# A transformer block on one core: the last head's norm by Newton steps, a conditioning row kept in a scratch row, and no separate square-root activation

## The chip, the core and the metric

The kernel runs on one core of one Trainium2 chip. The time is device microseconds of one execution; less is better. The engines are called as in the profile: PE multiplies matrices (PEld is its weight load), DVE and ACT do elementwise work, POOL does a little, SP issues the DMAs.

## The reference

One layer of a diffusion backbone: 512 latent tokens and 256 context tokens of width 1024. Everything is float32.

```python
mod = silu(c) @ w_mod + b_mod                 # six vectors of 1024: shift, scale, gate, twice
h   = rmsnorm(x) * (1 + sc1) + sh1            # the context the same, with c_ctx
# one projection of h feeds two mixers
o_mla  = attention of 4 heads over context + latent keys (128 plain + 64 rotary features)
o_hgrn = rmsnorm(forward scan + backward scan, 4 heads of 128) * silu(gate)
x = x + gt1 * (concat(o_mla, o_hgrn) @ w_out)
h2 = rmsnorm(x) * (1 + sc2) + sh2
x = x + gt2 * ((silu(h2 @ w_gate) * (h2 @ w_up)) @ w_down)
return rmsnorm(x) * g_final
```

## The kernel before

Features lie on the partitions and tokens along the free axis, except where a product needs it the other way. Each float32 operand is split into a rounded part and a remainder (`hi` and `lo`, `wh` and `wl`, and so on), and each product is three matmuls (`mm3`, lines 150 to 152). Weights arrive in units of 128x1024 through a ring of three buffers (`wf`); ACT casts a unit to `wh` (line 132) and DVE forms the remainder `wl` (line 133).

The stages follow each other: squares and norm of the inputs with the first two modulation vectors; the projection of the values; the low-rank attention features; four heads of the recurrence, each with two directions (`hgrn_dir`) and an output part (`hgrn_out`); the rotary key (`mla_kpe`, line 709); values, rotary queries and plain queries of the attention (`make_v`, `make_qr`, `make_q`, lines 770 to 803); the attention; the output projection; the second norm; the feed-forward part; the last norm.

The parts around the change:

- `rstd_cols` (line 184) makes 1/sqrt(mean + eps) of a few columns. With `fast=True` ACT takes the square root (line 190), DVE the reciprocal and one Newton step (lines 180 to 182). Otherwise DVE makes a first guess from the bits (lines 196 to 198) and takes three Newton steps.
- `hgrn_out(h)` adds up a head's output in PSUM (`po`), squares it on ACT (line 610), takes `rstd_cols`, with `fast` for the last head alone, and scales into `ow` (line 614), which PE transposes (line 620). ACT and DVE store the result as `onh` and `onl` (lines 622, 623).
- `late_mod` (line 422) makes the four later modulation vectors without PE: 32 rows of weights are fetched into the same `wf` ring (in the trace `wl<-in_wmt_dram`), and DVE multiplies each with silu(c) and sums (line 427). silu(c) lies on all partitions in `scx`, which is the place of the cosine and sine tables in `cs`. So it is made twice: once ahead of the recurrence (lines 433 to 435) for the first 12 rows; then the tables are loaded over it (line 746), and when the rotary queries are done, `c` is fetched again, goes through the sigmoid on ACT (line 814) and is multiplied on DVE (line 815).
- ACT needs a table for each of Exp, Sigmoid, Sqrt and Silu, and the compiler puts a table load (ACT_TABLE_LOAD) where the function changes. Copies, casts, scalings and squares need no load. Some small activations are there for their table alone, among them line 818 (Exp of one column), meant to stand ahead of the softmax, and line 1037 (Sqrt of one column), which stands in the code ahead of the last norm.
- The order in which an engine runs its instructions isn't the order of the code: a scheduler places each instruction on its engine's list by a priority, which follows the code, and by a model of when its inputs are there. Line 1037 depends on nothing late, so it lands in the middle of the program. Once the list is made, each engine works through it in order, and so does the DMA queue on SP.

Of the kernel before, what the change touches and what calls it, by code (L numbers as in the profile page):

```python
# [10 lines left out]
F32 = mybir.dt.float32  # L11
# [3 lines left out]
AF = mybir.ActivationFunctionType  # L15
# [3 lines left out]
P = 128  # L19
DM = 1024  # L20
# [4 lines left out]
NH = 4  # L25
# [27 lines left out]
def block_kernel(ctx: ExitStack, tc: tile.TileContext, xT, ctxT, vec, cin, cst, msk, wm, wmt, wi, wqkv, wo, wgu, wd, out):  # L53
    nc = tc.nc

    def pool(name, side, bufs=1):
        return tc.alloc_tile_pool(name=name, bufs=bufs, side=side, reuse_waits="tile")
# [4 lines left out]
    def nm(s):  # L62
        uid[0] += 1
        return f"{s}_{uid[0]}"
# [4 lines left out]
    def sm():  # L69
        return psum.tile([P, 512], F32, tag="sm", name=nm("sm"), bufs=4)  # L70
# [16 lines left out]
    epst = L0.tile([P, 1], F32, name="epst")  # L87
# [3 lines left out]
    epst2 = L0.tile([P, 1], F32, name="epst2")  # L91

    def V(name):
        a, b = VC[name]
        return vc[:, a:b]

    def C(name):
        a, b = CC[name]
        return cs[:, a:b]
# [44 lines left out]
    def unit(i, ahead=2):  # L144
        prefetch(i + 1 + ahead)
        return made[i]
# [12 lines left out]
    def tick(n=1):  # L159
        for _ in range(n):  # L160
            for g in list(side[:3]):
                if next(g, 1):
                    side.remove(g)
# [14 lines left out]
    def newton(r, t, v, n):  # L178
        for _ in range(n):
            nc.vector.tensor_mul(t, r, r)  # L180
            nc.vector.scalar_tensor_tensor(t, t, -0.5, v, op0=ALU.mult, op1=ALU.mult)
            nc.vector.scalar_tensor_tensor(r, t, 1.5, r, op0=ALU.add, op1=ALU.mult)

    def rstd_cols(tp, sums, dim, fast=False):
        src, n = sums
        v = tp.tile([P, 8], F32, tag="rs_v", name=nm("rsv"), bufs=2)[:, :n]
        t = tp.tile([P, 8], F32, tag="rs_t", name=nm("rst"), bufs=2)[:, :n]
        r = tp.tile([P, 8], F32, tag="rs_r", name=nm("rsr"), bufs=2)[:, :n]
        if fast:
            nc.scalar.activation(r, src, AF.Sqrt, bias=epst, scale=1.0 / dim)  # L190
            nc.vector.tensor_scalar(v, src, 1.0 / dim, EPS, op0=ALU.mult, op1=ALU.add)
            nc.vector.reciprocal(r, r)
            newton(r, t, v, 1)
        else:
            i = tp.tile([P, 8], I32, tag="rs_i", name=nm("rsi"), bufs=2)[:, :n]
            nc.vector.tensor_scalar(v, src, 1.0 / dim, EPS, op0=ALU.mult, op1=ALU.add)
            nc.vector.tensor_scalar(i, v.bitcast(I32), 1, None, op0=ALU.arith_shift_right)
            nc.vector.tensor_scalar(r.bitcast(I32), i, -1.0, float(0x5F3759DF), op0=ALU.mult, op1=ALU.add)
            newton(r, t, v, 3)
        return r, n  # L200
# [219 lines left out]
    scx = cs[:, CC["cos"][0] : CC["cos"][0] + DM]  # L420

    def late_mod(i):
# [5 lines left out]
        if i % 8 == 7:  # L428
            nc.vector.tensor_add(mod[:, i // 8, :], mod[:, i // 8, :], bm[:, 16 + i - 7 : 17 + i])

    HG = pool("HG", "left")
    scs = HG.tile([P, DM], F32, tag="U", name="scs", bufs=2)
    nc.sync.dma_start(scx, cin.rearrange("(o c) -> o c", o=1).to_broadcast([P, DM]))
    nc.scalar.activation(scs, scx, AF.Sigmoid)
    nc.vector.tensor_mul(scx, scx, scs)
    mk = HG.tile([P, 2, P], I32, name="mk")
    reset = HG.tile([P, 16, 33], BF16, name="reset")
    nc.gpsimd.memset(reset, 0.0)
    nc.gpsimd.memset(reset[:, :, 0:1], 1.0)
    nc.sync.dma_start(mk, msk)  # L440
    fc = HG.tile([P, NC + 2], F32, name="fc")
    nc.gpsimd.memset(fc, 1.0)
    am = []
    for j in range(2):
        t = HG.tile([P, 4, P], F32, name=f"am{j}")
        nc.gpsimd.memset(t, 0.0)
        am.append(t)
    zr = HG.tile([P, P], F32R, name="zr")
    nc.gpsimd.memset(zr.bitcast(F32), 0.0)
    zc = zr.bitcast(BF16)  # L450

    def project(u, lat=True, ctx_=True, ahead=2):
        w = unit(u, ahead)
        ps = big()
        for k in range(KT):
            L = sl(w, lambda t: t[:, k * P : (k + 1) * P])
            if lat:
                mm3(ps[:, 0, :], L, (hh[:, k, :], hl[:, k, :]), k == 0, k == KT - 1)
            if ctx_:
                mm3(ps[:, 1, :NC], L, (gh[:, k, :], gl[:, k, :]), k == 0, k == KT - 1)  # L460
            if k in ((1, 4) if ctx_ else (3,)):
                tick()
        return ps.rearrange("p a b -> p (a b)")
# [124 lines left out]
    def hgrn_out(h):  # L588
        while (h, 0) not in dirs or (h, 1) not in dirs or "hg" not in done:
            yield  # L590
        a2 = HG.tile([P, 4, P], F32, tag="a2", name=nm("a2"), bufs=1)
        nc.gpsimd.tensor_add(a2, am[0], am[1])
        for _ in range(3 if h % 2 else 1):
            yield
        po = sm()
        for j in range(4):
            t = po[:, j * P : (j + 1) * P]
            nc.tensor.matmul(t, a2[:, j, :], vt[:, j, h * P : (h + 1) * P], start=True, stop=False,  # L598
                             skip_group_check=True)
            for d in range(2):  # L600
                qg, U = dirs[h, d]
                for g in range(2):
                    c = 2 * j + g
                    nc.tensor.matmul(t[g * CH : (g + 1) * CH, :], qg[:, c, :], U[:, c, :], start=False,  # L604
                                     stop=(g == 1 and d == 1), skip_group_check=True, tile_position=(0, g * CH))
        done.add(h)
        sq = HG.tile([P, P], F32, tag="st", name=nm("osq"), bufs=1)
        ss = HG.tile([P, 4], F32, tag="rs_s", name=nm("oss"), bufs=1)
        for j in range(4):
            nc.scalar.activation(sq, po[:, j * P : (j + 1) * P], AF.Square, accum_out=ss[:, j : j + 1])  # L610
        rr, _ = rstd_cols(HG, (ss, 4), P, fast=h == NH - 1)
        w = HG.tile([P, 4, P], F32, tag="rs_d", name=nm("ow"), bufs=1)
        for j in range(4):
            nc.vector.scalar_tensor_tensor(w[:, j, :], po[:, j * P : (j + 1) * P], rr[:, j : j + 1],
                                           shg[:, j, h * P : (h + 1) * P], op0=ALU.mult, op1=ALU.mult)
        for _ in range(4):
            yield
        pt = sm()
        for j in range(4):
            nc.tensor.transpose(pt[:, j * P : (j + 1) * P], w[:, j, :], ident)  # L620
        gon = V("gon")[:, 0:1]
        nc.scalar.activation(onh[:, h, :], pt, AF.Copy, scale=gon)
        nc.vector.scalar_tensor_tensor(onl[:, h, :], pt, gon, onh[:, h, :].bitcast(F32), op0=ALU.mult,
                                       op1=ALU.subtract)
# [84 lines left out]
    def mla_kpe():  # L709
        ps = project(KPU)  # L710
        kp = HG.tile([P, NL], F32, tag="q", name=nm("kp"), bufs=2)
        m = HG.tile([P, NL], F32, tag="sg", name=nm("kpm"), bufs=2)
        nc.vector.tensor_mul(kp[0:64, :], ps[0:64, :NL], C("cos")[0:64, :])
        nc.vector.tensor_mul(kp[64:128, :], ps[64:128, :NL], C("sin")[64:128, :])
        nc.scalar.copy(m[0:64, :], kp[64:128, :])
        nc.vector.tensor_add(kp[0:64, :], kp[0:64, :], m[0:64, :])
        for src, c in ((ps[0:64, NL:NT], slice(NL, NT)), (kp[0:64, :], slice(0, NL))):
            for r in (slice(0, 64), slice(64, 128)):
                nc.scalar.copy(krh[r, c], src)
                nc.vector.tensor_sub(krl[r, c], src, krh[0:64, c].bitcast(F32))  # L720
# [13 lines left out]
    for h in range(NH):  # L734
# [8 lines left out]
        if h == 0:  # L743
            hg_pass()
            mods(12 - nm_[0])
            nc.sync.dma_start(cs[:, CC["cos"][0] :], cst[:, CC["cos"][0] :])
    mla_kpe()
    tick()
    B.release()
# [59 lines left out]
    for p in range(2):  # L809
        make_qr(p)  # L810
        tick()
    nc.sync.dma_start(scx, cin.rearrange("(o c) -> o c", o=1).to_broadcast([P, DM]))
    scs = HG.tile([P, DM], F32, tag="U", name="scs", bufs=2)
    nc.scalar.activation(scs, scx, AF.Sigmoid)
    nc.vector.tensor_mul(scx, scx, scs)
    lim_[0] = 32
    wq_n = unit(QU + 2, 1)
    nc.scalar.activation(epst2, scs[:, 0:1], AF.Exp)
    for h in range(NH):
        make_q(h)  # L820
        tick()
# [71 lines left out]
    for i in range(len(seq)):  # L893
# [10 lines left out]
        h, t = seq[i]  # L904
# [129 lines left out]
        for b in range(a, a + w, 256):  # L1034
            add_sq(b, x1[:, n, b : b + 256], n)

    nc.scalar.activation(epst2, epst, AF.Sqrt)

    def final(a):
        w = 256  # L1040
        dg = rstd_diag(N2, rstd_cols(N2, rstd_sums(sqa[a], w), DM, fast=True))
# [121 lines left out]
```

## Time and profile before

| what | value |
|---|---|
| median of three runs | 793.59 us (791.45 to 795.61) |
| the profiled execution | 792.62 us |
| its span in the trace | 790.8 us |
| granted PE clock | 0.988 |
| ACT table loads | 12, of 1283 ns each |

A row of a list in order of time reads: start in us from the span's beginning, duration, engine, line, operation, output<-input, shape, and in brackets how long the engine was idle before it and what ended that. Rows of one engine overlap by some hundredths of a microsecond, since the next starts before the last has written its end.

### The profile page before, as it was taken

To read this page: it belongs to the slowest core of one execution; us is meant where nothing else is said; L and a number is where in the kernel's file an instruction comes from. 1 tells how busy PE (TensorE), PEld (TensorE's weight loads), DVE (VectorE), ACT (ScalarE), POOL (GpSimd) and SP (SyncE) were. 2 spreads that over 40 slices of the span, in tenths; PEclk is the share of its full clock that TensorE was granted. 3 is DMA by queue.
4 is the path that set the end of the run, shared out by engine and by line. 5 is a ranking of instruction groups with operands and counts; after the bars stand their busy time and mean duration, and the time that the engine had idled before them with its cause. 6 is when DMAs were issued, how large, how long until landed. Compare 5 with 4: busy or idle time off the path is not lost.

```text
span 790.8 us, 10832 instructions
## 1 busy us (share of the span) xinstructions
PE 768.1 (97%) x4342; PEld 631.7 (80%) x4342; DVE 446.9 (57%) x820; ACT 311.4 (39%) x569; POOL 10.1 (1%) x18
## 2 busy tenths in 40 slices
PE   8899999999999989999999999999999999999995
PEld 7568878788887768888999888888888888888885
DVE  5576569839778989985566434432333233223324
ACT  6344246434544577664344223222322222212211
POOL 0000000000000100000000000000000000000000
PEclk8899999999999999999999999999999999999997
DMA  9923723311110022345403343423232323332303
GB/s 332 390 76 134 252 80 108 133 57 55 64 55 28 28 80 90 125 165 181 160 2 100 113 160 133 151 89 107 80 107 82 104 78 96 93 100 80 111 3 107
DMA packets 26706, 88.77 MB, mean 112 GB/s; under 512 B 2976, under 2 KB 5280, under 8 KB 26528
## 3 DMA queue, kind: packets, MB, share of 16 engines
q1 hardware_dynamic: 25568, 87.03, 33.0%
q10 hardware_dynamic: 1088, 1.05, 0.4%
q8 instruction: 34, 0.56, 0.3%
q14 instruction: 16, 0.13, 0.1%
HBM read 85.97 MB, written 2.10 MB: 111 GB/s over the span
## 4 chain that ended last, share of the span: by engine, by line
PE 89%; DVE 7%; ACT 2%; issue 1%; DMA 1%; SPq 0%; DVEq 0%; ACTq 0%
PE big L150 18%; PE big L151 17%; PE big L152 17%; PE sm L150 9%; PE sm L151 9%; PE sm L152 9%; PE big L857 2%; PE sm L604 1%; PE sm L876 1%; PE big L858 1%; PE sm L320 1%; DVE U L585 1%; PE sm L598 1%; DVE acl L309 1%; DVE G L506 1%
## 5 line engine op out<-in xcount | busy, mean ns | idle before, releaser
L133 DVE TENSOR_TENSOR wl<-wf,wh 128x1024 fp32r<-128x1024 f32 (+2 forms) x100 | 119.6, 1196 | 186.3 <-ACT wh L132 186.2
L132 ACT CAST wh<-wf 128x1024 fp32r<-128x1024 f32 (+2 forms) x100 | 102.9, 1029 | 280.3 <-PE big L151 167.6
L150 PE MATMUL big<-h2h,wh 128*128 128x512 f32 (+1 forms) x368 | 140.3, 381 | 0.0
L151 PE MATMUL big<-h2l,wh 128*128 128x512 f32 (+1 forms) x368 | 140.0, 381 | 0.0
L152 PE MATMUL big<-h2h,wl 128*128 128x512 f32 (+1 forms) x368 | 140.0, 381 | 0.0
L151 PEld LDWEIGHTS big<-h2l,wh 128*128 128x128 f32 x368 | 69.2, 188 | 14.6
L150 PEld LDWEIGHTS big<-h2h,wh 128*128 128x128 f32 x368 | 69.2, 188 | 14.4
L152 PEld LDWEIGHTS big<-h2h,wl 128*128 128x128 f32 x368 | 69.2, 188 | 14.4
L150 PE MATMUL sm<-ah,wh 128*128 128x512 f32 (+1 forms) x198 | 73.5, 371 | 0.0
L152 PE MATMUL sm<-ah,wl 128*128 128x512 f32 (+1 forms) x198 | 73.4, 371 | 0.0
L151 PE MATMUL sm<-al,wh 128*128 128x512 f32 (+1 forms) x198 | 73.4, 370 | 0.0
L427 DVE SCALAR_TENSOR_TENSOR wl<-wl,cs 128x1024 f32<-128x1024 f32 x32 | 39.0, 1220 | 33.8 <-DMA wl<-in_wmt_dram 33.8
L150 PE MATMUL big<-wh,hh 128*128 128x512 f32 x96 | 40.2, 422 | 3.3 <-ACT hh L340 1.9
L150 PEld LDWEIGHTS sm<-ah,wh 128*128 128x128 f32 x198 | 37.3, 188 | 7.1
L151 PEld LDWEIGHTS sm<-al,wh 128*128 128x128 f32 x198 | 37.3, 188 | 7.1
L152 PEld LDWEIGHTS sm<-ah,wl 128*128 128x128 f32 x198 | 37.3, 188 | 7.1
L150 PE MATMUL big<-hh,wh 128*128 128x512 f32 x104 | 42.8, 412 | 0.0
L151 PE MATMUL big<-hl,wh 128*128 128x512 f32 x104 | 40.9, 394 | 0.0
L152 PE MATMUL big<-hh,wl 128*128 128x512 f32 x104 | 40.8, 392 | 0.0
L151 PE MATMUL big<-wl,hh 128*128 128x512 f32 x96 | 38.8, 406 | 0.0
L152 PE MATMUL big<-wh,hl 128*128 128x512 f32 x96 | 38.4, 402 | 0.0
L506 DVE RECIPROCAL G<-S 128x528 f32<-128x528 f32 x8 | 27.5, 3432 | 0.1
(326 smaller groups left out, 1353.4 us busy)
## 6 DMA issues: line engine op xcount, KB each, us to landing
wf<-in_wgu_dram SPq DMA_DIRECT2D x44, 512.0 KB, 3.4
wl<-in_wmt_dram SPq DMA_DIRECT2D x32, 512.0 KB, 3.5
wf<-in_wi_dram SPq DMA_DIRECT2D x25, 512.0 KB, 3.9
wf<-in_wd_dram SPq DMA_DIRECT2D x16, 512.0 KB, 3.5
wms<-in_wm_dram SPq DMA_DIRECT2D x11, 512.0 KB, 9.6
wf<-in_wo_dram SPq DMA_DIRECT2D x8, 512.0 KB, 3.5
wf<-in_wd_dram SPq DMA_DIRECT2D x8, 384.0 KB, 3.1
wm<-in_wm_dram SPq DMA_DIRECT2D x5, 512.0 KB, 10.2
```

Source lines behind the costliest of these rows:

```text
L132: nc.scalar.copy(hi[:, :w], f[:, :w])
L133: nc.vector.tensor_sub(lo[:, :w], f[:, :w], hi[:, :w].bitcast(F32))
L150: nc.tensor.matmul(o, lh, rh, start=start, stop=False, skip_group_check=True)
L151: nc.tensor.matmul(o, lh, rl, start=False, stop=False, skip_group_check=True)
L152: nc.tensor.matmul(o, ll, rh, start=False, stop=stop, skip_group_check=True)
L309: nc.vector.tensor_add(acc_, acc_, sq_)
L320: nc.tensor.matmul(ps[32 * g : 32 * g + 32, :256], csil[:, 4 * j + kk, :], f[:, kk * 256 : (kk + 1) * 256], start=(j == 0), stop=(j == 1), ...
L427: nc.vector.scalar_tensor_tensor(f, f, 1.0, sc, op0=ALU.mult, op1=ALU.mult, accum_out=acc)
L506: nc.vector.reciprocal(I, S)
L585: nc.vector.scalar_tensor_tensor(U[:, c1, :], U[:, c0, :], er[:, 1, c0 : c0 + 1], U[:, c1, :], op0=ALU.mult, op1=ALU.add)
L598: nc.tensor.matmul(t, a2[:, j, :], vt[:, j, h * P : (h + 1) * P], start=True, stop=False, skip_group_check=True)
L857: nc.tensor.matmul(ps[:, 0, :], L, R[:, :NL], start=(i == 0), stop=(i == 4), skip_group_check=True)
```

## The change

Four edits:

1. The last head's norm takes the Newton form that the other heads have: no square root on ACT.
2. The row silu(c), made ahead of the recurrence, is stored into a scratch row in DRAM (`srow`), and later fetched from there to all partitions. The second sigmoid and its product on DVE go.
3. The Exp of one column moves from behind that sigmoid into `mla_kpe`, ahead of the casts of the rotary key. It now covers 64 partitions and reads `m`.
4. The Sqrt of one column ahead of the last norm goes.

```diff
+    srow = tc.dram_tile([1, DM], F32, name="srow")
     HG = pool("HG", "left")
     scs = HG.tile([P, DM], F32, tag="U", name="scs", bufs=2)
     nc.sync.dma_start(scx, cin.rearrange("(o c) -> o c", o=1).to_broadcast([P, DM]))
     nc.scalar.activation(scs, scx, AF.Sigmoid)
     nc.vector.tensor_mul(scx, scx, scs)
+    nc.sync.dma_start(srow, scx[0:1, :])
...
-        rr, _ = rstd_cols(HG, (ss, 4), P, fast=h == NH - 1)
+        rr, _ = rstd_cols(HG, (ss, 4), P)
...
         nc.vector.tensor_add(kp[0:64, :], kp[0:64, :], m[0:64, :])
+        nc.scalar.activation(epst2[0:64, :], m[0:64, 0:1], AF.Exp, scale=0.0)
         for src, c in ((ps[0:64, NL:NT], slice(NL, NT)), (kp[0:64, :], slice(0, NL))):
...
-    nc.sync.dma_start(scx, cin.rearrange("(o c) -> o c", o=1).to_broadcast([P, DM]))
-    scs = HG.tile([P, DM], F32, tag="U", name="scs", bufs=2)
-    nc.scalar.activation(scs, scx, AF.Sigmoid)
-    nc.vector.tensor_mul(scx, scx, scs)
+    nc.sync.dma_start(scx, srow.to_broadcast([P, DM]))
     lim_[0] = 32
     wq_n = unit(QU + 2, 1)
-    nc.scalar.activation(epst2, scs[:, 0:1], AF.Exp)
...
-    nc.scalar.activation(epst2, epst, AF.Sqrt)
-
```

The scheduler makes new lists for a part of the program, from `mla_kpe` to the end of the attention. Line numbers of the changed kernel are two or three higher there up to the reload, and one lower in the attention.

On DVE, at the last head's norm, before: `rsr` is the norm's factor, `rst` a Newton intermediate, `qnl` the remainder of a head's plain queries, `qs` the rotary queries, `wl` a weight remainder, `ow` the normalised head that PE transposes.

```order
L192 RECIPROCAL rsr_2719<-rsr_2719 128x4
L776 SCALAR_TENSOR_TENSOR qnl<-big_2762,qnh 128x512
L180 TENSOR_TENSOR rst_2718<-rsr_2719 128x4
L776 SCALAR_TENSOR_TENSOR qnl<-big_2771,qnh 128x512
L181 SCALAR_TENSOR_TENSOR rst_2718<-rst_2718,rsv_2717 128x4
L794 TENSOR_TENSOR qs<-m_383_2738,qs 64x512
L182 SCALAR_TENSOR_TENSOR rsr_2719<-rst_2718,rsr_2719 128x4
L794 TENSOR_TENSOR qs<-m_383_2738,qs 64x512
L614 SCALAR_TENSOR_TENSOR ow_2726<-sm_2690,rsr_2719,shg 128x128 x4
L815 TENSOR_TENSOR cs<-cs,scs 128x1024
L776 SCALAR_TENSOR_TENSOR qnl<-big_2787,qnh 128x512
L623 SCALAR_TENSOR_TENSOR onl<-sm_2780,vc,onh 128x512
```

The same place on DVE in the changed kernel; `wl_3517` in line 427 is a row of modulation weights, and `knl` is the remainder of the first head's keys.

```order
L779 SCALAR_TENSOR_TENSOR qnl<-big_2779,qnh 128x512
L180 TENSOR_TENSOR rst_2723<-rsr_2724 128x4
L133 TENSOR_TENSOR wl_3419<-wf_3416,wh_3418 128x1024
L181 SCALAR_TENSOR_TENSOR rst_2723<-rst_2723,rsv_2722 128x4
L779 SCALAR_TENSOR_TENSOR qnl<-big_2795,qnh 128x512
L182 SCALAR_TENSOR_TENSOR rsr_2724<-rst_2723,rsr_2724 128x4
L133 TENSOR_TENSOR wl_3425<-wf_3422,wh_3424 128x1024
L180 TENSOR_TENSOR rst_2723<-rsr_2724 128x4
L181 SCALAR_TENSOR_TENSOR rst_2723<-rst_2723,rsv_2722 128x4
L182 SCALAR_TENSOR_TENSOR rsr_2724<-rst_2723,rsr_2724 128x4
L616 SCALAR_TENSOR_TENSOR ow_2738<-sm_2695,rsr_2724,shg 128x128 x4
L625 SCALAR_TENSOR_TENSOR onl<-sm_2788,vc,onh 128x512
```

The first remainder (line 133) stood ahead of the reciprocal before and the second behind `knl`; now both, and the fourth `qnl`, stand ahead of `ow`. Right behind these rows, on DVE before:

```order
L623 SCALAR_TENSOR_TENSOR onl<-sm_2780,vc,onh 128x512
L769 TENSOR_TENSOR knl<-sm_2810,knh 128x512
L769 TENSOR_TENSOR knl<-sm_2819,knh 128x256
L133 TENSOR_TENSOR wl_3417<-wf_3414,wh_3416 128x1024
L861 TENSOR_REDUCE ast_2839<-big_2828 128x1
L861 TENSOR_REDUCE ast_2856<-big_2845 128x1
L427 SCALAR_TENSOR_TENSOR wl_3509,mod<-wl_3509,cs 128x1024
```

and in the changed kernel, `ast` being a row's maximum or its sum's reciprocal in the softmax:

```order
L625 SCALAR_TENSOR_TENSOR onl<-sm_2788,vc,onh 128x512
L427 SCALAR_TENSOR_TENSOR wl_3517,mod<-wl_3517,cs 128x1024
L772 TENSOR_TENSOR knl<-sm_2818,knh 128x512
L772 TENSOR_TENSOR knl<-sm_2827,knh 128x256
L860 TENSOR_REDUCE ast_2847<-big_2836 128x1
L427 SCALAR_TENSOR_TENSOR wl_3520,mod<-wl_3520,cs 128x1024
L863 RECIPROCAL ast_2847<-ast_2847 128x1
```

The first modulation product has moved from behind two row maxima to ahead of `knl`, and the second to ahead of the first reciprocal.

On ACT, in `mla_kpe` in the changed kernel (`krh` is the rotary key, `vh` a part of the values):

```order
L717 COPY kpm_2537<-kp_2536 64x512
L722 CAST krh<-big_2419 64x256
L719 ACT_TABLE_LOAD
L719 ACTIVATE epst_68<-kpm_2537 64x1
L722 CAST krh<-kp_2536 64x512
L722 CAST krh<-big_2419 64x256
L722 CAST krh<-kp_2536 64x512
L805 CAST vh<-big_2592 128x512
```

Before, the `vh` cast stood where the load and the Exp are now, and neither of these two was there.

## Prediction, made before the changed kernel was run

> **What bounds the kernel now.** I read the page first, then the busy time by stretches of 10 us, then the rows of PE, ACT and DVE in order of time in the one stretch that the edits touch.
>
> The page of the kernel before: span, PE's busy share, and the chain that ended last.
>
> ```profile
> span 790.8 us, 10832 instructions
> ...
> PE 768.1 (97%) x4342; PEld 631.7 (80%) x4342; DVE 446.9 (57%) x820; ACT 311.4 (39%) x569; POOL 10.1 (1%) x18
> ...
> PE 89%; DVE 7%; ACT 2%; issue 1%; DMA 1%; SPq 0%; DVEq 0%; ACTq 0%
> ```
>
> PE sets the time: what another engine does counts only where PE stands still for it. The stretches show where (the stretch and its length, then busy us and instructions of PE, PE's weight loads, DVE, ACT and POOL, the granted clock, the share of the DMA engines, GB/s):
>
> ```profile
> 285.00:295.00 10.00, 7.85 (x38) 5.41 (x35) 9.06 (x20) 9.39 (x19) 0.00 (x0) 1.00 0.36 116
> 295.00:305.00 10.00, 8.90 (x52) 7.61 (x51) 8.17 (x14) 8.73 (x16) 0.00 (x0) 1.00 0.17 63
> 305.00:315.00 10.00, 10.00 (x66) 8.97 (x65) 9.66 (x20) 7.14 (x18) 0.00 (x0) 1.00 0.30 97
> ```
>
> From 285 to 305 us, the hand-over from the last recurrence head to the attention, PE loses 2.15 + 1.10 = 3.25 us; behind it PE is full. So no edit here can gain much more than 3.3 us, 0.4% of the span. ACT and DVE are both near full there. PE's rows, with the idle time before each in brackets:
>
> ```profile
> 289.50 0.40 PE L152 MATMUL big<-cq,wl 128*128 128x512 f32 x1
> 290.65 0.51 PE L150 MATMUL big<-cq,wh 128*128 128x512 f32 x1 [0.75 <-DVE qnl L776]
> ...
> 291.92 0.40 PE L152 MATMUL big<-cq,wl 128*128 128x512 f32 x1
> 293.51 0.30 PE L620 MATMUL sm<-cs,ow 128*128 128x128 f32 x1 [1.19 <-DVE ow L614]
> ...
> 301.56 0.28 PE L152 MATMUL sm<-ck,wl 128*128 128x256 f32 x1
> 302.93 0.50 PE L857 MATMUL big<-knh,qnh 128*128 128x512 f32 x1 [1.10 <-ACT pp L863]
> ```
>
> PE starts a 512-wide matmul about every 0.23 us (a 256-wide one every 0.12), so in starts the three holes cost 0.92 (290.65 - 289.50 - 0.23), 1.36 and 1.25 us. The second waits for `ow`, the normalised last head.
>
> **The change, part by part.** ACT's rows there:
>
> ```profile
> 286.88 0.59 ACT L775 ACTIVATE qnh<-big 128x512 fp32r<-128x512 f32 x1
> 287.49 1.28 ACT L190 ACT_TABLE_LOAD   x1
> ...
> 288.99 0.58 ACT L775 ACTIVATE qnh<-big 128x512 fp32r<-128x512 f32 x1
> ...
> 291.23 1.28 ACT L814 ACT_TABLE_LOAD   x1
> 292.52 1.06 ACT L814 ACTIVATE scs<-cs 128x1024 f32<-128x1024 f32 x1
> ...
> 294.08 1.28 ACT L818 ACT_TABLE_LOAD   x1
> 295.38 0.20 ACT L818 ACTIVATE epst<-scs 128x1 f32<-128x1 f32 x1
> ...
> 296.78 1.08 ACT L132 CAST wh<-wf 128x1024 fp32r<-128x1024 f32 x1
> 297.88 1.28 ACT L1037 ACT_TABLE_LOAD   x1
> ...
> 300.60 1.28 ACT L863 ACT_TABLE_LOAD   x1 [1.22 <-DVE ast L861]
> ```
>
> Five table loads of 1.28 us (6.4 us) and the 1.06 us sigmoid leave this stretch. Two of the loads stand in front of PE's holes: that of L190 delays the second `qnh`, so `qnl`, so the hole at 290.65; that of L863 (the stray square root at L1037 has put the wrong table in) delays the first softmax and makes the hole at 302.93. Both holes should go: **-0.92 and -1.25 us**. The other three loads lie beside work of DVE and PE and free ACT alone.
>
> The Exp that now loads the table stands in `mla_kpe`:
>
> ```profile
> 266.31 0.62 ACT L715 COPY kpm<-kp 64x512 f32<-64x512 f32 x1 [0.93 <-DVE kp L714]
> 266.83 0.36 ACT L719 CAST krh<-big 64x256 fp32r<-64x256 f32 x1
> ...
> 269.03 0.62 ACT L719 CAST krh<-kp 64x512 fp32r<-64x512 f32 x1 [1.36 <-DVE kp L716]
> ```
>
> Load and Exp take 1.28 + 0.20 (the row at 295.38 is the same Exp at its old place) from 267.2 to 268.7; ACT waits for DVE's `kp` until 269.03, so they cost nothing, with 0.3 us to spare. The `vh` cast that stood in that gap goes behind the `krh` casts, 3 us later, still ahead of its DVE reader. Without that cover the 1.5 us would fall on `krl`, which PE waits for. [...]
>
> The Newton form and the order matter most. DVE before:
>
> ```profile
> 261.29 0.16 DVE L182 SCALAR_TENSOR_TENSOR rsr<-rst,rsr 128x4 f32<-128x4 f32 x1
> 261.49 0.16 DVE L180 TENSOR_TENSOR rst<-rsr 128x4 f32<-128x4 f32 x1
> ...
> 287.50 0.69 DVE L776 SCALAR_TENSOR_TENSOR qnl<-big,qnh 128x512 fp32r<-128x512 f32 x1 [0.32 <-ACT qnh L775]
> 288.11 0.68 DVE L789 TENSOR_TENSOR m<-m,m 128x512 f32<-128x512 f32 x1
> 288.71 1.22 DVE L133 TENSOR_TENSOR wl<-wf,wh 128x1024 fp32r<-128x1024 f32 x1
> ...
> 291.39 0.69 DVE L794 TENSOR_TENSOR qs<-m,qs 64x512 fp32r<-64x512 f32 x1
> ...
> 293.02 1.12 DVE L614 SCALAR_TENSOR_TENSOR ow<-sm,rsr,shg 128x128 f32<-128x128 f32 x4
> 294.06 1.21 DVE L815 TENSOR_TENSOR cs<-cs,scs 128x1024 f32<-128x1024 f32 x1
> ...
> 296.86 1.01 DVE L769 TENSOR_TENSOR knl<-sm,knh 128x512 fp32r<-128x512 f32 x2
> 297.89 1.23 DVE L133 TENSOR_TENSOR wl<-wf,wh 128x1024 fp32r<-128x1024 f32 x1
> ...
> 302.46 1.23 DVE L427 SCALAR_TENSOR_TENSOR wl<-wl,cs 128x1024 f32<-128x1024 f32 x1 [0.55 <-DMA wl<-in_wmt_dram]
> ```
>
> In the order before, `ow` stands behind three `qnl`, one weight remainder (L133), two `qs` and the short steps. In the new order all four `qnl` and both weight remainders stand ahead of it, between the Newton steps. DVE has no hole there, so I add: from 288.11, the `m` sum 0.6, three more `qnl` 1.8, two `qs` 1.4, two L133 2.3 and some nine short steps woven in at 0.08 to 0.1, then three dependent ones at 0.2 (the step between 261.29 and 261.49): 0.6 + 1.8 + 1.4 + 2.3 + 0.8 + 0.4 = 7.3 us, so `ow` starts at about 295.4 instead of 293.02, and PE's first transposition, 0.49 us behind it as in the rows above, at about 295.9. ACT doesn't hold it up: its weight cast (1.08) now stands ahead of the fourth `qnh`, both done by about 292.9. PE is through `make_q` at 291.1 and waits. **PE's second hole grows from 1.36 to about 4.7 us; at the transposition PE is late by 295.86 - 293.51 = 2.35 us, in which the 0.92 gained ahead of it is already counted.** The removed sigmoid product (1.21, behind `ow`) doesn't help `ow`.
>
> Next, the late-modulation product (L427) moves on DVE from behind the first two row maxima to ahead of `knl`. Its weights can be fetched only when the second L133 has freed their buffer (294.9), and the landing takes, with the slower case from an earlier stretch:
>
> ```profile
> wl<-in_wmt_dram SPq DMA_DIRECT2D x2, 512.0 KB, 3.3
> ...
> wl<-in_wmt_dram SPq DMA_DIRECT2D x8, 512.0 KB, 4.4
> ```
>
> so it can start at 298.2. DVE itself is free of `onl` at about 298.3 (transpositions, `onh`, `onl`, each right behind the other), so the product costs its own 1.2 us; `knl` is there at about 300.2. PE, with `make_k(0)` from 295.9 to 298.5 and 0.8 us of score matmuls that need `knh` alone, wants it at 299.3. **A new hole of about 0.9 to 1.0 us.** Before, three matmuls of `make_k(1)` stood there and `knl` was in time.
>
> The scratch row: the store to `srow` is queued on SP behind the product that makes it, ahead of weight loads.
>
> ```profile
> 68.80 1.22 DVE L435 TENSOR_TENSOR cs<-cs,scs 128x1024 f32<-128x1024 f32 x1
> ...
> 71.18 7.48 SPq L425 DMA_DIRECT2D wl<-in_wmt_dram  x5
> ```
>
> The product ends at 70.02, the next load behind it waits for another DVE step until 71.18 anyway; between 0 and the 0.33 us of an issue, I take 0. The reload has the same size, place and queue as before.
>
> Sum: +2.35 (with the -0.92 in it), +1.0, -1.25: **+2.1 us**. Behind it PE is full up to the end of the attention, and PE's order of the later stages stays. The profiled execution took 792.62 us (span 790.8), 1.0 under the median of the three runs, 793.59; I put the difference on the median: **795.7 us**. Bounds: `ow` could come 0.6 us earlier or later (the short steps at 0.08 or 0.2), the new hole lies between 0.7 (`onl` earlier) and 2.0 (landing 4.4), the gains between 1.25 and 2.17: +0.9 to +4.6.
>
> **The rivals.**
> 1. *Given back in the attention.* DVE is at 9.66 of 10 behind 305 us. One product of 1.22 us is now done ahead of the attention. If DVE paces PE there, most of the loss comes back: +0.9, 794.5 us. Against it: PE shows 10.00 in that stretch. Chance 0.17.
> 2. *The modulation fetches stall DVE* (the slow side). The products share one buffer, so each fetch starts when the product before it ends; in the new order the second stands ahead of the first reciprocal. If a landing takes 4.4 instead of 3.3 us, the first costs 1.1 us more, the next two about 0.6 each once they exceed the half microsecond that PE's transpositions have to spare: +2.1 + 2.3 = +4.4, 798.0 us. It decides from landings of about 3.9 us on. For it: eight landed at 4.4; against: those had seven weight loads for company. Chance 0.12.
> 3. [...] Chance 0.04.
> 4. *The ACT loads were what mattered.* If DVE gets through its list faster than the rows add up to, so that `ow` isn't later than before, the two holes close and nothing is lost: -0.92 - 1.25 = -2.2, 791.4 us. Against it: DVE's 7.3 us are added from rows. Chance 0.09.
>
> That the loads don't go is no case: the new order has none between `mla_kpe` and the second norm.
>
> **How the numbers follow.** The forecast keeps 0.58. The range takes in rivals 1, 3 and 4 and rival 2's point: 791.4 to 798.4 us. A measurement of this kernel can tell about 0.5%, 4 us: under 789.6 or over 797.6. No case reaches the first; I leave 0.03 for what I don't see. The second is rival 2 and a little of the forecast's upper bound: 0.13. Within: 0.84.
>
> **What would show it.** Right: no table load from 270 us to the second norm; PE's wait for `ow` at the transposition about 4.3 us instead of 1.19; a PE wait for `knl` near 1 us; no wait of PE for `pp` at the third score block; PE full behind. Wrong: `ow` at or before 293 us (rival 4); DVE waiting for `wl` by more than a microsecond (rival 2); a longer PE wait for `krl` (rival 3); new idle time of PE inside the attention.

## The result, and the profile after

The changed kernel takes 798.12 us, median of 9 runs (795.40 to 799.31), beside 792.75 us for the kernel before (9 runs, 790.59 to 795.61): a ratio of 1.0057, 95% interval 1.0039 to 1.0075. On a second chip it was 796.06 us (12 runs) against 793.68 (29 runs): 1.0040, interval 1.0014 to 1.0066. So it is slower, by about half a per cent: the forecast's sign, and more than its 2.1 us. The profiled execution took 798.16 us (span 796.4), the profiled one of before 792.62 (790.8).

Where do 5.6 us of span come from? I compare the two traces at two matmuls that both have: the one that waits for `krl`, ahead of everything that the change moves on PE, and one late in the feed-forward part. Before, then after:

```profile
270.96 0.50 PE L150 MATMUL big<-wh,ck 128*128 128x512 f32 x1 [1.64 <-DVE krl L720]
...
764.19 0.28 PE L152 MATMUL sm<-ah,wl 128*128 128x256 f32 x1
```

```profile
273.41 0.50 PE L150 MATMUL big<-wh,ck 128*128 128x512 f32 x1 [1.64 <-DVE krl L723]
...
770.17 0.28 PE L152 MATMUL sm<-ah,wl 128*128 128x256 f32 x1
```

The changed kernel's execution is 2.45 us late at the first and 5.98 at the second (the last 25 us take 0.4 of it back). So 3.53 us arise behind `krl`, where the edits to the order act, and 2.45 before it. The experiments show that the 2.45 belongs to that execution and not to the kernel; I call the difference of the two latenesses the kernel's *own* loss.

PE in the changed kernel where the own loss arises (start, length, line, and in brackets the idle time before it):

```profile
293.28 0.40 PE L152 MATMUL big<-cq,wl 128*128 128x512 f32 x1
298.49 0.49 PE L622 MATMUL sm<-cs,ow 128*128 128x128 f32 x2 [4.82 <-DVE ow L616]
...
300.04 0.63 PE L152 MATMUL sm<-ck,wl 128*128 128x512 f32 x1
300.47 0.63 PE L150 MATMUL sm<-ck,wh 128*128 128x512 f32 x1
300.89 0.63 PE L151 MATMUL sm<-ck,wh 128*128 128x512 f32 x1
...
303.91 0.50 PE L856 MATMUL big<-knl,qnh 128*128 128x512 f32 x1 [0.17 <-DVE knl L772]
```

The hole in front of the transposition is 4.82 us instead of 1.19. Behind it 512-wide matmuls start every 0.43 us instead of 0.23. The windows say why (stretch and length, busy us of PE, PEld, DVE, ACT, POOL, the granted clock, DMA share, GB/s):

```profile
295.49:298.90 3.41, 0.41 (x3) 0.38 (x3) 3.31 (x12) 0.00 (x0) 0.00 (x0) 1.00 0.52 161
298.90:302.31 3.41, 3.41 (x12) 2.83 (x12) 1.27 (x3) 1.01 (x2) 0.00 (x0) 0.50 0.43 147
302.31:305.72 3.41, 3.23 (x19) 2.63 (x18) 1.87 (x4) 0.64 (x2) 0.00 (x0) 1.00 0.40 114
```

For 3.41 us, right behind the hole, PE is given half its clock. Before has no such stretch between 25 and 780 us (1.00 in every 3.41 us of it). DVE in the changed kernel shows the list that makes the hole:

```profile
294.40 1.22 DVE L133 TENSOR_TENSOR wl<-wf,wh 128x1024 fp32r<-128x1024 f32 x1
...
295.61 0.68 DVE L779 SCALAR_TENSOR_TENSOR qnl<-big,qnh 128x512 fp32r<-128x512 f32 x1
296.21 0.15 DVE L182 SCALAR_TENSOR_TENSOR rsr<-rst,rsr 128x4 f32<-128x4 f32 x1
296.28 1.22 DVE L133 TENSOR_TENSOR wl<-wf,wh 128x1024 fp32r<-128x1024 f32 x1
...
298.00 1.12 DVE L616 SCALAR_TENSOR_TENSOR ow<-sm,rsr,shg 128x128 f32<-128x128 f32 x4
```

### The profile page after: what moved, and what is told of

Same layout as the page of the kernel before. It is cut to its first block, busy times and chain, and to the rows that moved or that the text cites. A ratio compares the mean times of both kernels' runs of the same rounds, so it can differ in the third digit from the quotient of the medians.

```text
span 796.4 us, 10832 instructions
## 1 busy us (share of the span) xinstructions
PE 770.2 (97%) x4342; PEld 632.7 (79%) x4342; DVE 446.3 (56%) x826; ACT 306.0 (38%) x562; POOL 10.1 (1%) x18
## 4 chain that ended last, share of the span: by engine, by line
PE 88%; DVE 7%; ACT 2%; issue 1%; DMA 1%; SPq 0%; DVEq 0%; ACTq 0%
PE big L150 17%; PE big L151 17%; PE big L152 17%; PE sm L150 9%; PE sm L151 9%; PE sm L152 9%; PE big L856 2%; PE sm L606 1%; PE sm L875 1%; PE big L857 1%; PE sm L320 1%; DVE U L587 1%; PE sm L600 1%; DMA xs<-in_xT_dram 1%; DVE G L508 1%
## 5 line engine op out<-in xcount | busy, mean ns | idle before, releaser
L133 DVE TENSOR_TENSOR wl<-wf,wh 128x1024 fp32r<-128x1024 f32 (+2 forms) x100 | 119.6, 1196 | 185.7 <-ACT wh L132 185.4
L427 DVE SCALAR_TENSOR_TENSOR wl<-wl,cs 128x1024 f32<-128x1024 f32 x32 | 39.0, 1221 | 34.2 <-DMA wl<-in_wmt_dram 34.2
L150 PEld LDWEIGHTS big<-wh,hh 128*128 128x128 f32 x96 | 18.3, 193 | 11.8 <-ACT hh L340 3.2
```

Of the source, the lines that this page charges most:

```text
L133: nc.vector.tensor_sub(lo[:, :w], f[:, :w], hi[:, :w].bitcast(F32))
L150: nc.tensor.matmul(o, lh, rh, start=start, stop=False, skip_group_check=True)
L427: nc.vector.scalar_tensor_tensor(f, f, 1.0, sc, op0=ALU.mult, op1=ALU.mult, accum_out=acc)
```

## The experiments

*The list theory*: the twelve dependent short steps of the norm (three for the guess, nine for the rounds) let long work in ahead of `ow` on DVE; PE's hole grows, and a hole of 4.8 us also costs clock (0.50 for 3.41 us). Two theories stand against it. *The start theory*: the scratch row or the moved Exp makes the first 30 us slower. *The table-load theory*: loads around the norm are what costs. All runs, the median beside that of the kernel before on the same chip, and the two latenesses against the trace of before (at 270.96 and at 764.19), whose difference is the own loss:

| kernel | us (runs) | before | ratio, 95% | late at `krl` | late at the end | own |
|---|---|---|---|---|---|---|
| changed | 798.12 (9) | 792.75 | 1.0039 to 1.0075 | 2.45 | 5.98 | +3.53 |
| changed, second | 796.06 (12) | 793.68 | 1.0014 to 1.0066 | 2.49 | 5.59 | +3.10 |
| changed, third | 797.43 (1) | 793.68 | - | 2.02 | 5.25 | +3.23 |
| square root kept | 793.66 (12) | 794.48 | 0.9988 to 1.0016 | 2.61 | 2.69 | +0.08 |
| Newton alone | 800.11 (6) | 794.48 | 1.0066 to 1.0107 | 3.43 | 7.57 | +4.14 |
| no stray load alone | 793.56 (12) | 794.48 | 0.9976 to 1.0011 | 0.53 | 0.14 | -0.39 |
| hole filled | 794.05 (12) | 793.68 | 0.9988 to 1.0037 | -1.54 | -0.26 | +1.28 |
| Newton on GpSimd | 793.92 (12) | 794.48 | 0.9974 to 1.0016 | 2.26 | 1.26 | -1.00 |
| the same, second | 793.38 (1) | 793.25 | - | 0.30 | 0.66 | +0.36 |
| norm on GpSimd | 794.42 (12) | 793.68 | 0.9987 to 1.0038 | 3.36 | 4.56 | +1.20 |
| the same, second | 793.84 (1) | 793.25 | - | 0.48 | 1.65 | +1.17 |
| norm there, `ow` later | 793.61 (12) | 793.25 | 0.9980 to 1.0021 | -0.92 | -1.45 | -0.53 |

**One edit undone.**

```
-        rr, _ = rstd_cols(HG, (ss, 4), P)
+        rr, _ = rstd_cols(HG, (ss, 4), P, fast=h == NH - 1)
```

> The changed kernel with one edit undone: the last head's norm by the square-root table again. DVE's list theory (the twelve dependent Newton steps let two weight remainders and the last qnl in ahead of ow; the 4.8 us hole that follows also halves the granted clock for 3.4 us): ow stands where it stood before, PE's wait at the transposition is back near 1.2 us, no stretch of granted clock 0.50 between 30 and 700 us, and the time is -0.5 to +0.7 us of the kernel before. Start theory (the scratch row or the moved Exp makes the first 30 us 2.4 us slower, by which the changed kernel's trace is late at 30 us): that lateness stays, +1.9 to +3.0 us. Table-load theory (loads around the norm are what costs): two loads are back beside the norm, +2.6 us over the changed kernel, so near +8 us.

```profile
PE sm L622 <- DVE ow L616: 1.2, 1, 1.2
PE big L856 <- ACT pp L862: 1.1, 1, 1.1
```

These are its longest waits of PE behind `krl` (two of 0.7 follow, for `ptl` and `qnl`): what it waited for, us in total, how often, the longest. They are those of the kernel before, and so is the time: own loss 0.08, ratio 1.0002. The whole loss is the Newton form's, though this kernel has the scratch row and the moved Exp. Its own trace is 2.61 us late at `krl` while its median is that of before: the lateness of the start theory is there and costs the median nothing. The table-load theory falls too: the loads beside the norm are back, and nothing is lost.

**That edit alone, on the kernel before.**

```
-        rr, _ = rstd_cols(HG, (ss, 4), P, fast=h == NH - 1)
+        rr, _ = rstd_cols(HG, (ss, 4), P)
```

> The kernel before with one edit alone: the last head's norm by Newton steps; sigmoid, reload and stray load stay. DVE's list theory: ow stands behind both weight remainders, all qnl and the conditioning product (1.21 us more than in the changed kernel), PE's hole is near 5.9 us, the granted clock falls to 0.50 for about 3.4 us behind it; +4 to +7 us over the kernel before, and no lateness at 30 us. Start theory: no scratch row, so no lateness at 30 us, and only the 2 to 3 us of the hole. Table-load theory: one load less ahead of the second qnh, -0.9 us.

```profile
296.65 1.22 DVE L815 TENSOR_TENSOR cs<-cs,scs 128x1024 f32<-128x1024 f32 x1
...
298.53 1.21 DVE L133 TENSOR_TENSOR wl<-wf,wh 128x1024 fp32r<-128x1024 f32 x1
...
300.05 1.13 DVE L614 SCALAR_TENSOR_TENSOR ow<-sm,rsr,shg 128x128 f32<-128x128 f32 x4
```

```profile
300.55 0.66 PE L620 MATMUL sm<-cs,ow 128*128 128x128 f32 x2 [5.82 <-DVE ow L614]
```

One edit of four gives +4.14, more than the whole change: the product that the reload removes, 1.22 us, now stands on the list too; a hole of 5.82, and half clock behind it (0.50 from 299.96, for 3.41 us). By medians it is +5.2 to +8.5 us, more than its own loss; six runs alone, so I rest on the trace. This trace is 3.43 us late at `krl` without any scratch row: against the start theory again.

**No stray load, alone.**

```
-    nc.scalar.activation(epst2, epst, AF.Sqrt)
```

> The kernel before with the stray square-root load removed alone. DVE's list theory and table-load theory alike: PE's hole of 1.25 us in front of the third score block closes and nothing else moves, -1.2 us. If another wait stood right behind it (the row maximum of the next block, the fetch of the modulation row): 0. Lateness at 30 us: none by any theory.

The hole at the third score block is gone: against before, PE is 0.53 us late at `krl`, 0.64 early at its 1941st matmul (304.48 instead of 305.12), which makes -1.17. But 0.14 late at the end leaves -0.39: by 360 us two thirds of the gain are given back, in pieces of which the trace names one wait, 0.24 us for `ptl` at 319.00. It looks like the prediction's first rival, seen on the gain; what paces PE there isn't shown.

**The hole filled with matmuls that nobody reads.**

```
+NFILL = 18
...
+        if h == NH - 1:
+            for _ in range(NFILL):
+                nc.tensor.matmul(pb[:, 1, :], cqh[:, 1, :P], cqh[:, 1, :], start=True, stop=True, skip_group_check=True)
```

> The changed kernel with 18 extra 512-wide matmuls (4.1 us at 0.23) behind the last make_q, their results unused, so that PE works through most of the hole in which it waits for ow. Clock theory (the 1.4 us that the changed kernel loses beyond its waits come from the half clock that follows the hole): no granted clock of 0.50 near 300 us, make_k(0)'s matmuls start every 0.23 us instead of 0.43, and, since ow itself is no earlier than 0.6 us, the kernel is 1 to 2 us faster than the changed one: +2 to +4.5 us of the kernel before by medians, about +1.3 to +2.3 us from the last recurrence head on in its trace. Rival (the slow matmuls have another cause: their operands, the transpositions between them, a shared memory port): spacing 0.43 stays and the time is that of the changed kernel or up to 4 us longer.

```profile
289.52 4.24 PE L782 MATMUL big<-cq 128*128 128x512 f32 x18
294.03 0.30 PE L623 MATMUL sm<-cs,ow 128*128 128x128 f32 x1 [0.27 <-DVE ow L617]
...
295.44 0.40 PE L152 MATMUL sm<-ck,wh 128*128 128x512 f32 x1
295.67 0.39 PE L153 MATMUL sm<-ck,wl 128*128 128x512 f32 x1
```

```profile
294.00:297.40 3.40, 3.37 (x19) 2.78 (x20) 2.53 (x7) 2.04 (x4) 0.00 (x0) 1.00 0.60 195
```

Eighteen more matmuls make the kernel faster: +1.28 instead of +3.10 to +3.53, the clock stays at 1.00 and the spacing at 0.23. Some 0.5 us of the 1.8 to 2.3 is `ow` itself, which stands ahead of the last `qnl` here (lateness at the transposition 2.06 instead of 2.54); the rest goes with the clock, and the same matmuls on the same operands are no longer slow, so those operands aren't the cause.

**The changed kernel twice more.**

> The changed kernel once more, unaltered, beside the kernel before on another chip. Start theory: late by about 2.4 us at 30 us again, +5 us in all. Free-running clock theory (the granted clock is decided in steps of 3.41 us that begin at another point of each execution, so that the slow stretch of the first 30 us lasts 10.2, 13.7 or 17.1 us whatever the kernel): the lateness at 30 us is any of about +0.5, +2.4 or +3.5 us; the part behind it is +2.5 to +3.5 us in every execution with a hole near 4.8 us, of which 1.4 us only if one of the steps falls wholly or nearly so into the hole.

> The changed kernel a third time, one look. As for the second: hole at the transposition 4.7 to 4.9 us; whether the clock of 0.50 follows it depends, by the free-running clock theory, on where its steps of 3.41 us fall, by the rival (a fixed delay behind the last matmul) it follows each time.

Each has the hole of 4.8 us, 0.50 behind it (from 298.96 and from 298.05), and +3.10 and +3.23. Their lateness at `krl`, 2.49 and 2.02, is what the start theory expects too, so these two don't decide it. All thirteen traces together do. The slow stretch of the first 30 us lasts 6.83, 10.24, 13.65 or 17.07 us, which are 2 to 5 steps of 3.41, and the lateness follows it whatever the kernel: -1.54 and -0.92 with two steps, 0.00 (before itself) to 0.53 with three, 2.02 to 2.61 with four, 3.36 and 3.43 with five. With five it is 3.43 without the scratch row and 3.36 with it. What sorts them is where the borders of the steps fall. Taking whole steps off the end of the slow stretch leaves a border 0.2 to 0.8 us behind the span's start in the four traces with three slow steps, 1.1 to 2.0 in the five with four, 2.85 and 2.99 in the two with five, 3.03 and 3.41 in the two with two. The trace of before had three, all three of the changed kernel four. Before, then the changed kernel:

```profile
20.00:24.00 4.00, 4.00 (x15) 2.16 (x15) 1.10 (x3) 0.11 (x1) 0.00 (x0) 0.50 1.02 409
24.00:27.00 3.00, 3.00 (x26) 1.52 (x25) 1.41 (x5) 0.93 (x2) 0.00 (x0) 0.97 1.03 411
```

```profile
20.00:24.00 4.00, 3.93 (x14) 2.19 (x15) 1.49 (x3) 0.49 (x2) 0.00 (x0) 0.50 1.01 405
24.00:27.00 3.00, 3.00 (x16) 1.74 (x15) 1.23 (x4) 0.22 (x1) 0.00 (x0) 0.50 1.02 407
```

**The Newton rounds on GpSimd**, which is idle there in the changed kernel: the same rounds with `nc.gpsimd`, each in four steps where DVE takes three, for the last head alone.

```
-        rr, _ = rstd_cols(HG, (ss, 4), P)
+        rr, _ = rstd_cols(HG, (ss, 4), P, e=nc.gpsimd if h == NH - 1 else None)
```

> The changed kernel with the three Newton rounds of the last head on GpSimd, so that DVE's list isn't opened between dependent steps: ow stands behind two qnl and two qs alone. DVE's list theory: if one GpSimd step on 128x4 takes 0.1 to 0.3 us (twelve of them 1.2 to 3.6 us), PE's hole at the transposition is under 1.5 us, the clock stays at 1.00, and the time is -2.6 to -0.5 us of the kernel before; if a step takes 0.6 us or more (7 us in all), ow comes as late as in the changed kernel, +2 to +5 us. Start theory: +2.4 us on top in either case. Table-load theory: as the first case whatever GpSimd takes.

> The kernel with the Newton rounds alone on GpSimd, one more look. Free-running clock theory: its hole of 2.5 us costs the clock only if more than about half of one 3.41 us step falls into it: no 0.50 stretch if the step border cuts the hole near its middle, as in the first look, else one of 3.41 us (+1.4 us or less). Fixed-delay rival: none, as in the first look.

The same kernel, two executions. Two steps of the clock in the first, then two in the second:

```profile
291.80:295.22 3.42, 1.69 (x8) 1.08 (x6) 1.33 (x2) 2.69 (x4) 2.72 (x9) 1.00 0.01 2
295.22:298.63 3.41, 2.64 (x16) 2.20 (x16) 2.86 (x7) 1.25 (x2) 2.49 (x4) 1.00 0.00 0
```

```profile
290.96:294.37 3.41, 0.91 (x5) 0.49 (x4) 1.08 (x5) 1.60 (x3) 2.69 (x10) 1.00 0.00 0
294.37:297.78 3.41, 3.41 (x12) 2.69 (x11) 2.24 (x5) 1.01 (x2) 1.49 (x3) 0.50 0.00 0
```

PE waits 2.5 us for `ow` in both. Where the border of a step cuts the hole, PE is busy for 1.69 us of the one step and 2.64 of the next, and the clock stays; where the hole lies in one step, with 0.91 us of work, the next runs at 0.50. A half clock at a fixed delay behind the last matmul would have come in both or in neither, so that rival falls. The price between the two is 0.36 + 1.00 = 1.36 us.

```profile
291.75 1.40 DVE L803 TENSOR_TENSOR qs<-m,qs 64x512 fp32r<-64x512 f32 x2
```

```profile
291.49 0.20 POOL L182 TENSOR_TENSOR rst<-rst,rsv 128x4 f32<-128x4 f32 x1
291.78 0.72 POOL L183 TENSOR_SCALAR rst<-rst 128x4 f32<-128x4 f32 x1
292.58 0.64 POOL L184 TENSOR_TENSOR rsr<-rsr,rst 128x4 f32<-128x4 f32 x1
293.30 0.20 POOL L181 TENSOR_TENSOR rst<-rsr 128x4 f32<-128x4 f32 x1
```

The twelve GpSimd steps take 4.25 us (291.21 to 295.46 in the first execution) where 1.2 to 3.6 were expected, so the hole is 2.5 us and not under 1.5. They are 0.28 apart but for two of 0.7 to 0.8, and none of DVE's long work stands in between; the first execution's gain of 1.00 us is that of the list theory, at its small end.

**The whole norm on GpSimd**, guess included.

```
-            nc.vector.tensor_scalar(v, src, 1.0 / dim, EPS, op0=ALU.mult, op1=ALU.add)
-            nc.vector.tensor_scalar(i, v.bitcast(I32), 1, None, op0=ALU.arith_shift_right)
-            nc.vector.tensor_scalar(r.bitcast(I32), i, -1.0, float(0x5F3759DF), op0=ALU.mult, op1=ALU.add)
...
+            q = e or nc.vector
+            q.tensor_scalar(v, src, 1.0 / dim, EPS, op0=ALU.mult, op1=ALU.add)
+            if e is not None:
+                e.tensor_scalar(r.bitcast(I32), v.bitcast(I32), -0.5, float(0x5F3759DF), op0=ALU.mult, op1=ALU.add)
...
```

> A candidate to beat both: the changed kernel with the whole norm of the last head, guess too (without its shift), on GpSimd: 14 steps at 0.28 us, 3.9 us from the end of the sums of squares, with nothing of DVE's list between them. DVE's list theory: ow stands behind one qnl alone and starts near 293.4 us minus the lateness of the start, 2 us earlier than with GpSimd from the guess on; the transpositions go ahead of the fourth make_q, and PE's hole there falls below 1.5 us and mostly vanishes from the sum: -3.5 to -1.2 us of the kernel before. If GpSimd's steps take 0.7 us beside DVE's long ones: 0 to +2.

> The kernel with the whole norm on GpSimd, one more look. Free-running clock theory: its hole of 2.0 us is followed by a 0.50 stretch only if the hole lies nearly whole in one step, as in the first look, else not. Fixed-delay rival: the stretch is there again, 1.2 us behind the end of the hole.

```profile
292.99:296.40 3.41, 1.42 (x8) 0.99 (x8) 1.70 (x6) 1.04 (x3) 2.75 (x9) 1.00 0.02 6
296.40:299.81 3.41, 3.41 (x10) 2.63 (x9) 3.31 (x6) 0.88 (x2) 0.73 (x1) 0.50 0.00 0
```

`ow` is as early as expected: it starts at 294.70, 0.8 us earlier than in the kernel with the rounds alone on GpSimd (295.49), in a trace that is 1.1 us later at `krl`. The time is a miss: the transposition now stands ahead of the fourth `make_q`, so PE asks for it that much sooner and waits 2.0 us, and in both executions these lie in one step, with 1.42 and 1.45 us of work: half clock, +1.20 and +1.17. The idea that the hole would mostly vanish from the sum is wrong.

**The products of `ow` pushed back**, so that PE works on meanwhile.

```
+            with prio(-150 if h == NH - 1 else 0):
                 nc.vector.scalar_tensor_tensor(w[:, j, :], po[:, j * P : (j + 1) * P], rr[:, j : j + 1],
...
```

> A second candidate: the whole last norm on GpSimd as in the first, and the normalising products on DVE pushed back, so that PE does the fourth make_q and most of make_k(0) before it asks for ow. DVE's list theory: GpSimd's 4.3 us pass beside PE's work, no PE wait for ow above 0.5 us, no granted clock of 0.50 near 300 us, and of the 3.5 us of holes in the kernel before 2 to 3.5 go: -3.5 to -2.0 us from the last recurrence head on in its trace, -4 to -1 us by medians. Rival (give-back: the attention is paced by DVE, as the removal of the stray load alone suggests, which was 1.15 us ahead at 305 us and 0.4 at the end): the lead at 305 us is there, and most of it is gone by 345 us, -1 to 0 us.

```profile
PE sm L633 <- DVE ow L627: 1.8, 1, 1.8
...
PE big L867 <- ACT pp L873: 0.6, 1, 0.6
```

The wait is a miss too: the scheduler drew the first of the four products forward, with its transposition, into the fourth `make_q`, and PE still waits 1.8 us. The clock stays at 1.00, as expected. The own gain is 0.53 us, and 0.46 of it is there at 306 us (a matmul at 305.80 beside 307.18), so nothing is given back here. No version here is faster than the kernel before by more than the measurements can tell.

## Why the prediction was right, and where it was not

- *PE late by 2.35 us at the transposition*: 298.49 - 293.51 - 2.44 (the lateness of this execution ahead of it) = 2.54, and in the second and third trace the same. `ow` stands behind four `qnl` and both L133, as read from the order. The hole is 4.98 in starts (298.49 - 293.28 - 0.23) for "about 4.7", and 4.82 of idle time for "about 4.3".
- *The 1.25 us at the third score block*: PE no longer waits for `pp`. Right, and -1.17 when done alone.
- *The Exp in `mla_kpe` costs nothing*: the load and the Exp (269.65 to 271.15) leave ACT 0.32 us of waiting for `kp`, and PE's wait for `krl` is 1.64 in both traces. *The store to the scratch row*: nothing that shows, by the kernel that has it and is as fast as before (ratio 0.9988 to 1.0016).
- *"A new hole of about 0.9 to 1.0 us" for `knl`*: 0.17. The prediction took `make_k(0)` at full clock. At half clock PE asks for `knl` 2.0 us later than it said (301.30 without the lateness, beside 299.3), and `knl` comes 1.3 us later (301.47 beside 300.2), so this wait is covered by a larger loss. What it would be at full clock isn't shown: in the filled kernel L427 stands behind `knl`.
- *What failed*: the sum had no term for the clock. The prediction took the 0.23 us spacing as PE's price behind any hole. Behind the hole of 4.8 us the granted clock was 0.50 for 3.41 us; PE, busy all through it, started a 512-wide matmul every 0.43 us instead of 0.23, so I estimate that up to half of the 3.41 us, 1.7, are lost (1.36 between the two executions of the kernel with the rounds on GpSimd). With it the sum closes: 2.54 + 1.7 - 1.25 + 0.17 = 3.16, against +3.10 to +3.53. The missing 1.7 is partly hidden in the total, since the wait for `knl` was priced 0.8 us too high.
- *Rival 1* (given back in the attention): not in the changed kernel, whose own lateness is 310.81 - 305.12 - 2.45 = 3.24 at PE's 1941st matmul and 3.53 at the end, but something like it is at work on the gain of the stray load. *Rival 2*: DVE waits 0.69 and 0.25 us for the two fetches, which land in 3.3 to 3.6 us, under the 3.9 from which it was to decide; it isn't what added the rest. *Rival 3* (a longer wait of PE for `krl`): neither trace shows a table load longer than 1.28 us; the Exp began 0.02 us behind the moved one, and the wait stayed at 1.64. *Rival 4*: no sign.
- *The trace of before as a base*: it had three slow steps at its start and the changed kernel's four. Of the 5.6 us between the spans 2.4 are this, and a forecast can't hold them; the two intervals of the ratio, 3.1 to 5.9 and 1.1 to 5.2 us, both hold the own loss of 3.1 to 3.5.
- *The range*: 798.12 us lies in it by 0.3 us, and above 797.6, the case that was given 0.13 and put down to rival 2. The upper end comes from that rival and from the forecast's own bound of +4.6 (with `ow` 0.6 us later and a landing of 4.4 us); none of this happened. So the sign and the wait for `ow` were understood, and that the time falls inside the range is in part luck. The lower bound of +0.9 doesn't follow from its terms, which give 2.35 - 0.6 + 0.7 - 1.25 = 1.2; nothing hangs on it.

## What to carry to other kernels

The chain of twelve dependent steps of 0.15 to 0.17 us on a busy engine wasn't paid here by its own durations but by what the scheduler filled in between (PE's hole went from 1.19 to 4.82 us): read the order, and price the consumer's wait by everything that now stands ahead. A wait of PE had a second price here beyond its length: between 286 and 300 us, a step of 3.41 us with 1.45 us of PE work or less in it was followed by one at half clock. Compare two traces at a matmul ahead of the change and one far behind it: that told own losses to half a us where the clock fell alike, while the medians of a dozen runs left 1 to 2 us on either side open.

## What the runs showed of the hardware

- The granted clock changed in steps of 3.41 us (slow stretches of 6.83 to 17.07 us in the first 30 us, of 3.41 behind the holes), and the borders of the steps lay at another point of each execution. Between 286 and 300 us, a step with 0 to 0.42, 0.91, 1.42 or 1.45 us of PE work was followed by one at 0.50. One with 1.69 us was not, nor, in the changed kernel, was the step from 292.08 to 295.49 with 1.60 (1.58 in its second trace). So in these traces what made the difference lies between 1.45 and 1.58 us of a step, or 42% to 46%. This doesn't hold for the first 30 us: in the trace of before a step with 2.45 us of work (10.53 to 13.94) was followed by 0.50. The matmuls there are others, most of them narrower, and what decides isn't shown.
- The same kernel therefore paid 1.36 us more in one execution than in another, with the same hole of 2.5 us.
- PE's first 30 us hold 2 to 5 such slow steps, by where the border of the steps falls: 5 us between the extremes of thirteen traces (-1.54 to 3.43). In the 29 runs of the kernel before on the second chip, time and mean granted clock go together (correlation -0.97; allowing for the clock, the scatter falls from 2.4 to 0.5 us). So most of what scatters goes with the granted clock; run by run it isn't shown that this lies in the first 30 us.
- GpSimd took 0.28 us from step to step on 128x4, and 0.7 to 0.8 us for one or two that ran beside a TENSOR_TENSOR of DVE (`qs`, `m`); beside a `qnl`, it stayed at 0.28.
